# Hybrid transformer layer on one core: context keys' norm first, the merged sum's differences tile by tile, gate's rows beside another merge

## Chip, cores and metric

One core of a Trainium2 chip runs the whole kernel in one launch. Its engines work side by side, each through its own queue in order: TensorE (PE, matrix products into PSUM banks), VectorE (DVE), ScalarE (ACT), GpSimd (POOL) and SyncE (SP, which issues most DMAs). An instruction starts when those ahead of it in its queue have started and its semaphores are up, so a waiting instruction holds up all behind it. The metric is the device time of one execution in microseconds (us); smaller is better.

## What is computed

One layer over 1024 latent tokens of width 1024, with 256 context tokens as further keys. One projection feeds three branches: A, neighbourhood attention of 8 heads of 64; B, a short gated convolution; C, a Conformer convolution module with a layer norm. The branches are merged by sigmoid gates, projected and added to the input:

```python
h, gate = modulate(x, c, norm_g, w_ada, b_ada)      # gate: last third of silu(c) @ w_ada + b_ada
z = h @ w_in
kc, vc = na_kv(hc @ w_in[:, A_K:A_Z], k_norm_g)     # kc: RMS norm of the context keys, per head
...
ga, gb, gc = split(sigmoid(z[..., GATES:]), 3)
m = ga * (ya @ w_out_a) + gb * (yb @ w_out_b) + gc * (yc @ w_out_c)
x = x + gate * (m @ w_o)
```

All of it is float32. A product of two float32 matrices is made from three products of rounded parts: each operand is split into hi (a cast, on ACT) and lo (what the cast left out, a subtraction on VectorE or POOL), and hi·hi, hi·lo and lo·hi are summed in PSUM.

## The kernel before

**Order.** The program is traced in Python; when it is built, a planner puts each engine's instructions in an order by its own estimates, in which an instruction may move past others unless something holds it. `tc.issue_after(x)` is such a hold: what is traced inside it stands behind x on x's engine. Where generators are stepped beside a loop (`next(...)`), the place of tracing sets roughly where the work ends up.

**Start of attention** (about 100 to 130 us). `qkv(hp)` projects queries, keys and values of a pair of heads in eight images of 128 tokens (`ps`), and `context()` those of the 256 context tokens in two tiles (`psc`). `norm` squares a tile on ACT (`sqh`), sums it on VectorE (`ssh`), takes the power -1/2 on POOL (`rsqrt_mean`, L75 and L76) and scales on VectorE (`tm`, for the context `tmc`, L221). TensorE transposes the scaled keys (`pskc`, L194), ACT makes `kcT` of them. `attend(hp)` then prepares a head in `stacks`: VectorE's casts and differences of queries (`qd`, `qlz`, L500 to L502) and keys (`ks`, L506), `kc` of the context, and `vs` of the values (L508, POOL). POOL also fills zeros into `qlz` and `pbuf` (L481, L487), makes the low parts of the context's values (`vc`, L200) and the biases (L534). The first `qkv` runs ahead of attention, and the second, `qkv(1)`, whose images and context products TensorE computes between the first heads' scores (`sl`, `sc`), right behind the first `attend`.

**Merges** (911 us to the end). `merge(br, ys, beside)` computes for each of eight row tiles dm and two halves b a product `ops` of 12 matmuls and adds it, times the branch's gate `gs`, into `m`, held as `mt[dm]`. The order is B, A, C. Beside B's merge (`beside_b`) run A's products with its gate path (`a_steps`) and the first part of the conformer's layer norm (`norm_steps`: 32 matmuls `sums`, with the splits `lnh` and `lnl`); beside A's (`beside_a`) its end: TensorE spreads the reciprocal deviation over the partitions (`rstd`, L1113), and for each of four tiles VectorE, ACT and POOL make `cvin` (L1125) and `zcin` (L1127), split into `ych` and `ycl`, which C's merge multiplies. Beside C's merge runs `gate_steps`: one row of the condition is loaded and passed through silu (`cr`, `crs`, L1137 and L1138), and for eight tiles `gw` of the gate's weights VectorE multiplies by `crs` and sums along the row into one column of `gate` (L1143). `gs`, `zcin`, `cr`, `crs` and `gw` share eight buffers (`big`).

**m times w_o** follows C's merge in seven products per pair of row tiles instead of eight (Strassen's scheme, in Winograd's form), so sums and differences of blocks are needed. Of m: `M11`, `MT1` and `M21` inside the merge, and `MT2`, `MT3`, `M22`, `MT4` in `m_sums`, which for each of four j makes three differences `mraw` on VectorE and four splits `mb`, the cast on ACT, the low part on VectorE. Of w_o: `s1` to `s4` on POOL, and the splits `wh`, `wl`. `fin_first(n)`, a generator, makes the products `fa` and `fc` and keeps them: `pv` is a copy of `fa` on ACT (L1224), and `fc + pv` on VectorE (L1229); its second step adds `M21`'s product onto `fa`, for which the bank must have been copied, and puts the result out (`o`, L1213). `fin_rest(n)` makes `ff` (from `MT2`), `fe` (`M22`) and `fd` (`MT3`, `MT4`). `ops`, `fa`, `fc`, `ff`, `fe` and `fd` share six PSUM banks.

Of the kernel before, what the change touches and what calls it, by code (L numbers as in the profile page):

```python
# [8 lines left out]
F32 = mybir.dt.float32  # L9
F32R = mybir.dt.float32r  # L10
BF16 = mybir.dt.bfloat16
AF = mybir.ActivationFunctionType
ALU = mybir.AluOpType
AX = mybir.AxisListType
# [7 lines left out]
L = 256  # L22
EPS = 1e-6
HD = 64
# [16 lines left out]
def tile_hybrid(ctx: ExitStack, tc, x, xT, cx, cond, crow, ng, w_ada, b_ada, wqkv, wz,  # L41
                wout, wo, qg, kg, rpbs, mask, cs, cf, cfb, lng, lnb, out):
    nc = tc.nc
    pe, act, dve, pool = nc.tensor, nc.scalar, nc.vector, nc.gpsimd
# [19 lines left out]
    half_neg = cst.tile([P, 8], F32, name="half_neg")  # L64
# [8 lines left out]
    def rsqrt_mean(dst, ss, n, k):  # L73

        pool.tensor_scalar(out=dst, in0=ss, scalar1=1.0 / n, scalar2=EPS, op0=ALU.mult, op1=ALU.add)  # L75
        pool.tensor_tensor(out=dst, in0=dst, in1=half_neg[:, :k], op=ALU.pow)  # L76


    def split_chunk(src, n, lo_eng, raw=None):
# [43 lines left out]
    state = {"wp": wp}  # L123
    qg8 = cst.tile([P, 1], F32, name="qg8")
    kgn = cst.tile([P, 1], F32, name="kgn")

    def qkv(hp, w=None, cts=None, first=(), psc=None, mid=None):
# [3 lines left out]
        kcT = a1.tile([P, L], F32, tag="kcT", name="kcT")  # L131
# [37 lines left out]
        def context():  # L169
            if not state["vc"]:  # L170
                a1.tile([P, 2 * L], F32R, tag="cht", name="cht", bufs=4)
            state["vc"] = 1
            vc = [a1.tile([P, 2, P], F32R, tag=f"vc{h}", name="vc") for h in range(2)]
            pc = psc or [ps_m.tile([P, 512], F32, tag="m", name="psc"), ps_q.tile([P, 512], F32, tag="q", name="psc")]
            for k in range(KT):
                if cts:
                    cht = cts[k // 2][:, k % 2]
                else:
                    cht = a1.tile([P, 2 * L], F32R, tag="cht", name="cht", bufs=4)
                    nc.sync.dma_start(cht.bitcast(F32), chd[k])  # L180
                wh, wl = w[k][0][:, 128:384], w[k][1][:, 128:384]
                for t in range(2):
                    o = pc[t][:, :256]
                    a, b = cht[:, t * P : t * P + P], cht[:, L + t * P : L + t * P + P]
                    pe.matmul(o, a, wh, start=k == 0, stop=False)
                    pe.matmul(o, a, wl, start=False, stop=False)
                    pe.matmul(o, b, wh, start=False, stop=k == KT - 1)  # L187
            pst_ = ps_q.tile([P, 512], F32, tag="q", name="pskc")
            for t in range(2):
                tm = a1.tile([P, 256], F32, tag="tm", name="tmc", bufs=5)  # L190
                raw = a1.tile([P, 384], F32, tag="raw", name="rawc", bufs=3)
                act.copy(raw[:, :256], pc[t][:, :256])
                norm(raw[:, :P], tm[:, :P], 2)
                pe.transpose(out=pst_[:, t * P : (t + 1) * P], in_=tm[:, :P], identity=ident)  # L194
                for h in range(2):
                    hs = slice(h * HD, h * HD + HD)
                    hi, lo = vc[h][:, t, hs], vc[h][:, t, HD - h * HD : P - h * HD]
                    src = raw[:, P + h * HD : P + h * HD + HD]
                    act.copy(hi, src)
                    pool.tensor_tensor(out=lo, in0=src, in1=hi.bitcast(F32), op=ALU.subtract)  # L200
            act.activation(kcT, pst_[:, :L], AF.Identity, scale=kgn)
            return vc

        if mid:
# [9 lines left out]

    def norm(ps, dst, n):
        sq = a1.tile([P, 256], F32, tag="sqh", name="sqh", bufs=1)
        act.activation(sq[:, : n * HD], ps, AF.Square)
        ss = cst.tile([P, 4], F32, tag="ssh", name="ssh", bufs=3)
        dve.tensor_reduce(out=ss[:, :n], in_=sq[:, : n * HD].rearrange("p (h d) -> p h d", d=HD), axis=AX.X, op=ALU.add)
        rsqrt_mean(ss[:, :n], ss[:, :n], HD, n)  # L220
        dve.tensor_tensor(out=dst.rearrange("p (h d) -> p h d", d=HD), in0=ps.rearrange("p (h d) -> p h d", d=HD),  # L221
                          in1=ss[:, :n].rearrange("p (h o) -> p h o", o=1).broadcast_to([P, n, HD]), op=ALU.mult)
# [41 lines left out]
    with tc.tile_pool(name="st", bufs=1) as st, tc.tile_pool(name="ps_t", bufs=1, space=PSUM) as pst:  # L264
# [121 lines left out]
        for k in range(KT):  # L386
            raw = tmp("wraw")[:, :384]
# [77 lines left out]
    with tc.tile_pool(name="at", bufs=1, reuse_waits="tile") as at, \  # L465
# [4 lines left out]
        for hf in range(2):  # L470
            m = mka[:, hf]
            for i in range(3):
                o, n = TYPE_OFF[i], (288, 384, 288)[i]
# [10 lines left out]
        for i in range(4):  # L484
            t = at.tile([P, 768], F32, name=f"pbuf{i}")
            pad = t[:, :512].rearrange("p (j m) -> p j m", j=4)
            pool.memset(pad[:, :, 96:] if i % 2 == 0 else pad[:, :, :32], 0.0)  # L487
            pbuf.append(t)

        def stacks(hp, h):  # L490
# [104 lines left out]
        def h_sums(j):  # L595
# [16 lines left out]
            b21 = whole(0, 4 + j)  # L612
            less(3, b21, t1)

        for hp in range(4):
            attend(hp)
            if hp < 3:
                qkv(hp + 1, w1 if hp == 0 else None)
            if hp < 3:
                for j in ((), (0,), (1,))[hp]:  # L620
                    h_sums(j)
                glu(hp + 1)
# [425 lines left out]
    yc_s = []  # L1048
# [109 lines left out]
    def beside_b(dm, b):  # L1158
        if dm < 2:
            a_parts.append(a_load(2 * dm + b))  # L1160
        else:
            next(asteps, None)
        for _ in range(3 if dm > 1 else 0):
            next(steps, None)

    def beside_a(dm, b):
        for _ in range(2):
# [3 lines left out]
    merge(0, ya_s, beside_a)  # L1171
    for _ in steps:
        pass
    merge(2, yc_s, lambda dm, b: next(gsteps, None))
    for _ in gsteps:
        pass


    def m_sums():
        for j in range(4):  # L1180
            t1, b12 = halves(mt[j])
            b21, b22 = halves(mt[4 + j])
            raw = [tmp("mraw") for _ in range(3)]
            sub(dve, raw[0], b22, t1)
            sub(dve, raw[1], b22, b12)
            sub(dve, raw[2], b21, raw[0])
            for blocks, t, r in ((MT2, t2, raw[0]), (MT3, t3, raw[1])):
                blocks[j] = t[j]
                split(*t[j], r, dve)
            for blocks, tag, r in ((M22, j, b22), (MT4, 4 + j, raw[2])):  # L1190
                blocks[j] = halves(hp_pool.tile([P, S], F32R, tag=f"ha{tag}", name="mb"))
                split(*blocks[j], r, dve)
# [25 lines left out]
    def fin_first(n):  # L1218

        a11, a12, a21, a22 = w_rows(n)  # L1220
        a = fin_bank("fa")
        product(a, wsplit(a11, pool), M11, True, True)
        p1, v = held[n] = halves(big("pv"))
        act.copy(p1, a)  # L1224
        s1 = w_sum("s1", a21, a22, ALU.add)
        w12 = wsplit(a12, pool)
        c = fin_bank("fc")
        product(c, wsplit(s1, pool), MT1, True, True)
        dve.tensor_tensor(out=v, in0=c, in1=p1, op=ALU.add)  # L1229
        yield  # L1230
        xr = ltmp("xr0")
        nc.sync.dma_start(xr, xT[2 * n][:, B512[0]])
        product(a, w12, M21, False, True)
        put(2 * n, 0, a, xr)
# [28 lines left out]
    firsts = [fin_first(n) for n in range(4)]  # L1263
    for n in (0, 1):
        next(firsts[n])
    m_sums()
    for n in (0, 1, 2, 2, 3, 3):
        next(firsts[n], None)
    for n in range(4):
        fin_rest(n)  # L1270

# [83 lines left out]
```

## Time and profile before

| | us |
|---|---|
| median of three runs | 1156.2 |
| fastest, slowest run | 1153.46, 1156.84 |
| the profiled execution | 1154.55 |
| its span, first to last instruction | 1152.7 |
| TensorE busy in it | 1100.0 (95%) |
| VectorE, POOL, ACT busy | 893.1, 668.2, 569.2 |

The profile is one execution. "Idle before" an instruction is the time its engine stood still ahead of it, with the instruction that ended the wait behind the arrow. Matmuls are pipelined: one shown as 0.39 us starts 0.23 us after the one ahead of it. PEclk is the granted TensorE clock as a share of 2.4 GHz; at 1.2 GHz a matmul of 512 columns starts 0.43 us after the one ahead.

### The profile page before, as it was taken

How to read it: one execution, taken by the hardware profiler on the slowest of the kernel's cores; microseconds unless marked ns; L12 is line 12 of the kernel's file. 1: busy time of each engine (PE TensorE's matmuls, PEld its weight loads, DVE VectorE, ACT ScalarE, POOL GpSimd, SP SyncE). 2: the span in 40 equal slices, each digit the busy share in tenths (PEclk: the TensorE clock that was granted, in tenths of full speed). 3: DMA queues.
4: the chain of work that ended last, by engine and by line, in shares of the span. 5: the costliest groups of instructions: out<-in, count | busy, mean ns of one | idle time of the engine just before them, and what ended most of it. 6: DMA issues, size and time to landing. Idle time of an engine off the chain costs nothing.

```text
span 1152.7 us, 16450 instructions
## 1 busy us (share of the span) xinstructions
PE 1100.0 (95%) x5506; PEld 939.0 (81%) x5506; DVE 893.1 (77%) x1560; ACT 569.2 (49%) x1154; POOL 668.2 (58%) x611
## 2 busy tenths in 40 slices
PE   7889898999999999998999999999999999989698
PEld 5768796998999788887888888888888788878586
DVE  6976478878868885654996898897992587799975
ACT  6755366567557588784433233323434453413420
POOL 2255656446546953311968677877776645952870
PEclk7999999999999999999999999999999999999899
DMA  9536222323322323117233434344437953681263
GB/s 352 208 103 200 89 69 68 123 84 89 105 82 79 118 88 117 62 49 272 84 113 126 127 111 135 121 133 151 128 128 287 377 223 110 201 301 63 81 202 119
DMA packets 79510, 163.65 MB, mean 142 GB/s; under 512 B 10049, under 2 KB 29249, under 8 KB 79425
## 3 DMA queue, kind: packets, MB, share of 16 engines
q1 hardware_dynamic: 74816, 160.50, 41.0%
q10 hardware_dynamic: 4608, 2.10, 0.6%
q8 instruction: 43, 0.70, 0.3%
q14 instruction: 43, 0.34, 0.1%
HBM read 120.62 MB, written 41.94 MB: 141 GB/s over the span
## 4 chain that ended last, share of the span: by engine, by line
PE 71%; DVE 17%; ACT 4%; POOL 4%; issue 4%; DMA 1%; SPq 0%; ACTq 0%; POOLq 0%; DVEq 0%
PE ga L720 3%; PE gd L720 3%; PE ga L721 3%; PE gd L721 3%; PE gd L722 3%; PE ga L722 3%; PE zaps L106 3%; PE zaps L104 3%; PE zaps L105 3%; PE pp L565 2%; PE ps L106 2%; PE ps L104 2%; PE ps L105 2%; DVE mb L644 2%; PE ops L104 2%
## 5 line engine op out<-in xcount | busy, mean ns | idle before, releaser
L696 DVE SCALAR_TENSOR_TENSOR cv<-upad,cf_t,cv 128x512 f32<-128x512 f32 x240 | 167.0, 746 | 0.1
L534 POOL TENSOR_TENSOR bias<-mka,vimg 128x288 f32<-128x288 bf16 (+1 forms) x64 | 56.9, 890 | 85.7 <-DVE mn L548 81.3
L644 POOL TENSOR_TENSOR wl<-s,wh 128x512 fp32r<-128x512 f32 x69 | 98.6, 1444 | 13.8 <-ACT wh L643 13.0
L643 ACT CAST wh<-s 128x512 fp32r<-128x512 f32 x92 | 55.8, 616 | 96.1 <-POOL s L647 66.1
L87 POOL TENSOR_TENSOR wl<-wr,wh 128x384 fp32r<-128x384 f32 (+1 forms) x57 | 56.8, 1003 | 54.0 <-ACT wh L85 53.2
L570 DVE TENSOR_TENSOR plo<-pp,ph 128x512 fp32r<-128x512 f32 (+1 forms) x96 | 60.6, 639 | 7.8 <-ACT ph L568 7.1
L550 ACT ACTIVATE pbuf<-sc,mn 128x256 f32<-128x256 f32 x64 | 30.4, 476 | 73.0 <-DVE mn L548 71.5
L644 POOL TENSOR_TENSOR wl<-wr,wh 128x512 fp32r<-128x512 f32 x44 | 60.6, 1378 | 4.2 <-ACT wh L643 4.2
L565 PE MATMUL pp<-ident,pbuf 128*128 128x128 f32 x352 | 59.0, 273 | 4.0 <-DVE pbuf L554 2.8
L552 DVE TENSOR_TENSOR mn<-mn 128x1 f32<-128x1 f32 x64 | 20.0, 312 | 53.3 <-ACT pbuf L551 53.1
L720 PE MATMUL ga<-ha,wh 128*128 128x512 f32 x152 | 59.2, 390 | 1.2 <-ACT wh L643 1.2
L568 ACT CAST ph<-pp 128x512 fp32r<-128x512 f32 (+1 forms) x96 | 51.6, 549 | 15.9 <-PE pp L565 15.2
L721 PE MATMUL ga<-ha,wh 128*128 128x512 f32 x152 | 59.1, 389 | 0.0
L722 PE MATMUL ga<-ha,wl 128*128 128x512 f32 x152 | 59.1, 389 | 0.0
L565 PEld LDWEIGHTS pp<-ident,pbuf 128*128 128x128 f32 x352 | 42.6, 140 | 10.2 <-DVE pbuf L554 5.2
L748 POOL TENSOR_TENSOR s<-wr 128x512 f32<-128x512 f32 x16 | 23.3, 1454 | 38.7 <-DMA wr<-in_wz 33.3
L76 POOL TENSOR_TENSOR ssh<-ssh,half_neg 128x4 f32<-128x4 f32 (+1 forms) x40 | 41.7, 1044 | 2.9
L909 ACT ACTIVATE c<-c 128x512 f32<-128x512 f32 x18 | 11.4, 632 | 60.1 <-DVE c L726 44.5
L85 ACT CAST wh<-wr 128x384 fp32r<-128x384 f32 (+1 forms) x66 | 31.1, 486 | 18.6 <-PE psc L187 10.0
L106 PE MATMUL ps<-wh,hb 128*128 128x384 f32 x112 | 38.2, 344 | 1.2 <-DVE hb L336 1.1
L104 PE MATMUL ps<-wh,hb 128*128 128x384 f32 x112 | 38.7, 346 | 0.5 <-ACT hb L330 0.5
L548 DVE CUSTOM_DVE_ANT_0 pbuf<-sl,bias,mn 128x288 f32<-128x288 f32 (+1 forms) x64 | 36.1, 564 | 3.5 <-PE sl L543 0.4
(425 smaller groups left out, 4061.0 us busy)
## 6 DMA issues: line engine op xcount, KB each, us to landing
wr<-in_wz SPq DMA_DIRECT2D x34, 512.0 KB, 3.9
gs<-gd SPq DMA_DIRECT2D x24, 512.0 KB, 5.0
wada<-in_w_ada SPq DMA_DIRECT2D x16, 512.0 KB, 8.7
wrf<-in_wo SPq DMA_DIRECT2D x16, 512.0 KB, 4.1
wr<-in_wz SPq DMA_DIRECT2D x36, 192.0 KB, 2.5
cht<-chd SPq DMA_DIRECT2D x24, 256.0 KB, 2.9
wro<-in_wout SPq DMA_DIRECT2D x24, 256.0 KB, 4.4
gd<-gate SPq DMA_DIRECT2D x22, 256.0 KB, 3.6
```

The costliest lines, as they stand in the source:

```text
L87: lo_eng.tensor_tensor(out=lo[:, :n], in0=raw[:, :n], in1=hi[:, :n].bitcast(F32), op=ALU.subtract)
L104: pe.matmul(ps, ah, bh, start=i == 0, stop=False)
L105: pe.matmul(ps, ah, bl, start=False, stop=False)
L106: pe.matmul(ps, al, bh, start=False, stop=i == n - 1)
L534: pool.tensor_tensor(out=bv, in0=mv, in1=iv, op=ALU.subtract)
L565: pe.transpose(out=pp[:, c * 256 + hf * P : c * 256 + hf * P + P], in_=pts[hf][:, o : o + P], identity=ident)
L570: dve.tensor_tensor(out=plo[:, : m * 256], in0=pp[:, : m * 256], in1=ph[:, : m * 256].bitcast(F32), op=ALU.subtract)
L644: eng.tensor_tensor(out=lo, in0=src, in1=hi.bitcast(F32), op=ALU.subtract)
L696: dve.scalar_tensor_tensor(out=acc[b], in0=src, scalar=cf_t[:, i, j : j + 1], in1=acc[b], op0=ALU.mult, op1=ALU.add)
L720: pe.matmul(ps, wh, bh, start=first and j == 0, stop=False, skip_group_check=True)
L721: pe.matmul(ps, wh, bl, start=False, stop=False, skip_group_check=True)
L722: pe.matmul(ps, wl, bh, start=False, stop=last and j == 3, skip_group_check=True)
```

## The change

Nothing is added to or taken from the arithmetic: every engine has the same work, in another order, and the order in the middle of the kernel, from about 290 to 910 us, is the same.

```diff
@@ rsqrt_mean, norm: remember the last power, sum and square
-        pool.tensor_tensor(out=dst, in0=dst, in1=half_neg[:, :k], op=ALU.pow)
+        state["pow"] = pool.tensor_tensor(out=dst, in0=dst, in1=half_neg[:, :k], op=ALU.pow)
...
@@ context()
+            raws = []
             for t in range(2):
                 ...
                 pe.transpose(out=pst_[:, t * P : (t + 1) * P], in_=tm[:, :P], identity=ident)
+                raws.append(raw)
+            state["kc"] = state["pow"], state["red"], state["sq"]
+            act.activation(kcT, pst_[:, :L], AF.Identity, scale=kgn)
+            for t, raw in enumerate(raws):
                 for h in range(2):
                     ...
                     act.copy(hi, src)
-                    pool.tensor_tensor(out=lo, in0=src, in1=hi.bitcast(F32), op=ALU.subtract)
-            act.activation(kcT, pst_[:, :L], AF.Identity, scale=kgn)
+                    with tc.issue_after(state["kc"][0].ins):
+                        pool.tensor_tensor(out=lo, in0=src, in1=hi.bitcast(F32), op=ALU.subtract)
@@ attention
-            pool.memset(pad[:, :, 96:] if i % 2 == 0 else pad[:, :, :32], 0.0)
+            with tc.issue_after(state["kc"][0].ins):
+                pool.memset(pad[:, :, 96:] if i % 2 == 0 else pad[:, :, :32], 0.0)
...
+        with tc.issue_after(state["kc"][0].ins), tc.issue_after(state["kc"][1].ins), tc.issue_after(state["kc"][2].ins):
+            attend(0)
         for hp in range(4):
-            attend(hp)
+            if hp:
+                attend(hp)
@@ beside_b, merges
+        if dm > 2 or dm + b == 3:
+            next(gsteps, None)
...
-    merge(2, yc_s, lambda dm, b: next(gsteps, None))
     for _ in gsteps:
         pass
+    merge(2, yc_s)
@@ m_sums
-    def m_sums():
-        for j in range(4):
+    def m_sums(j):
+        with tc.issue_after(state["fin"].ins):
...
-        act.copy(p1, a)
+        state["fin"] = act.copy(p1, a)
...
-    m_sums()
-    for n in (0, 1, 2, 2, 3, 3):
-        next(firsts[n], None)
+    for j, ns in enumerate(((0, 1), (2,), (2, 3), (3,))):
+        m_sums(j)
+        for n in ns:
+            next(firsts[n], None)
```

So the two context tiles' squares, sums and powers go ahead of the first head's preparation on ACT, VectorE and POOL; gate's rows go from C's merge to the second half of B's; and the m_sums of tile j are held on ACT behind the copy `pv` that was traced last, and lie between the steps of `fin_first`.

POOL at the start of attention, before (ssh with L75 and L76 are the steps of the norm's power; the first pair is the context's):

```order
L487 MEMSET pbuf_1351 128x4x32
L200 TENSOR_TENSOR vc<-rawc,vc 128x64 x2
L534 TENSOR_TENSOR bias<-mka,vimg 128x288
L200 TENSOR_TENSOR vc<-rawc,vc 128x64 x2
L534 TENSOR_TENSOR bias<-mka,vimg 128x288
L534 TENSOR_TENSOR bias<-mka,vimg 128x384
L75 TENSOR_SCALAR ssh<-ssh 128x2
L508 TENSOR_TENSOR vs<-vb,vs 128x8x64 x2
L87 TENSOR_TENSOR wl<-wr,wh 128x384
L76 TENSOR_TENSOR ssh<-ssh,half_neg 128x2
```

and POOL at the same place now:

```order
L486 MEMSET qlz_1343 64x1024
L75 TENSOR_SCALAR ssh<-ssh 128x2
L76 TENSOR_TENSOR ssh<-ssh,half_neg 128x2
L87 TENSOR_TENSOR wl<-wr,wh 128x384
L75 TENSOR_SCALAR ssh<-ssh 128x2
L76 TENSOR_TENSOR ssh<-ssh,half_neg 128x2
L206 TENSOR_TENSOR vc<-rawc,vc 128x64 x4
L493 MEMSET pbuf_1345 128x4x32
```

Both powers moved ahead of vc, pbuf, bias and vs.

VectorE in B's merge, at the first half of dm=3, before:

```order
L1032 TENSOR_TENSOR mt_10068<-ops_10069,gs_10066 128x512
L644 TENSOR_TENSOR lnl_10177<-sq_10174,lnh_10176 128x512
L1032 TENSOR_TENSOR mt_10068<-ops_10102,gs_10066 128x512
L644 TENSOR_TENSOR wl_10563<-wro_10503,wh_10562 128x512
L644 TENSOR_TENSOR lnl_10183<-sq_10180,lnh_10182 128x512
L1032 TENSOR_TENSOR mt_10132<-ops_10133,gs_10130 128x512
```

and now (the ISA rows with gw are gate's, the others among them read the sum out):

```order
L1041 TENSOR_TENSOR mt_10075<-ops_10076,gs_10073 128x512
L1152 ISA gw_10067,gate_9901<-gw_10067,crs_10064 128x1024
L1152 ISA gate_9901 128x1
L1152 ISA gw_10110,gate_9901<-gw_10110,crs_10064 128x1024
L1152 ISA gate_9901 128x1
L1152 ISA gw_10134,gate_9901<-gw_10134,crs_10064 128x1024
L1152 ISA gate_9901 128x1
L653 TENSOR_TENSOR lnl_10193<-sq_10190,lnh_10192 128x512
L1041 TENSOR_TENSOR mt_10075<-ops_10112,gs_10073 128x512
```

Three of gate's eight rows stand ahead of the first lnl of the squares, the other five behind it; the layer norm's rows come that much later. In C's merge TensorE's order follows: before, the 21st to 24th matmul, with the last tile's parts (ych_10585, ycl_10586) in the second half of dm=0,

```order
L106 MATMUL ops_10799<-ych_10529,wl_10772 128x512
L104 MATMUL ops_10799<-ych_10585,wh_10771 128x512
L105 MATMUL ops_10799<-ycl_10586,wh_10771 128x512
L106 MATMUL ops_10799<-ych_10585,wl_10772 128x512
L104 MATMUL ops_10830<-ych_10414,wh_10824 128x512
```

and now the 38th to 42nd, behind most of dm=1 (the last tile's parts are ych_10615 and ycl_10616, and ops_10822 is dm=0's second half):

```order
L104 MATMUL ops_10822<-ych_10615,wh_10801 128x512
L105 MATMUL ops_10865<-ycl_10501,wh_10844 128x512
L106 MATMUL ops_10865<-ych_10500,wl_10845 128x512
L105 MATMUL ops_10822<-ycl_10616,wh_10801 128x512
L106 MATMUL ops_10822<-ych_10615,wl_10802 128x512
```

The last tile's products moved 16 to 18 matmuls back. ACT around the first copies pv, before (mb<-mraw are casts of m_sums):

```order
L643 CAST mb_11143<-mraw_11257 128x512
L643 CAST mb_11140<-mraw_11272 128x512
L643 CAST wh_11363<-wrf_11338 128x512
L643 CAST mb_11135<-mt_10345 128x512
L643 CAST wh_11368<-s1_11361 128x512
L1224 COPY pv_11167<-fa_11150 128x512
```

and now:

```order
L652 CAST wh_11336<-s1_11329 128x512
L1235 COPY pv_11167<-fa_11150 128x512
L652 CAST wh_11391<-wrf_11386 128x512
L652 CAST wh_11411<-wrf_11386 128x512
L1235 COPY pv_11214<-fa_11197 128x512
L652 CAST mb_11138<-mraw_11240 128x512
```

The two copies moved ahead of every cast of mraw. VectorE behind C's merge now, where before all mraw rows stood ahead of the first o:

```order
L1240 TENSOR_TENSOR pv_11214<-fc_11222,pv_11214 128x512
L653 TENSOR_TENSOR mb_11253<-mraw_11242,mb_11253 128x512
L1224 SCALAR_TENSOR_TENSOR o_11270<-fa_11150,gate_9901,xr0_11256 128x512
L1224 SCALAR_TENSOR_TENSOR o_11287<-fa_11197,gate_9901,xr0_11273 128x512
L656 TENSOR_TENSOR mraw_11290<-mt_10213,mt_9943 128x512
L656 TENSOR_TENSOR mraw_11291<-mt_10213,mt_9943 128x512
```

From mraw_11290 it is 24 rows to mb_11141, the low part of MT2's last tile.

## Rows read from the trace of the kernel before

**Rows 1.** TensorE's waits by releaser, 100 to 300 us: total us, times, longest

```profile
PE pskc L194 <- DVE tmc L221: 2.6, 1, 2.6
...
PE sl L542 <- DVE ks L506: 1.2, 1, 1.2
```

**Rows 2.** TensorE's waits by releaser, 900 us to the end

```profile
PE fa L720 <- ACT pv L1224: 8.6, 2, 5.4
PE ops L105 <- DVE ycl L644: 3.1, 1, 3.1
PE fa L721 <- DVE mb L644: 1.0, 1, 1.0
PE fd L720 <- DVE o L1213: 0.9, 1, 0.9
```

**Rows 3.** stretches: length, busy PE, PEld, DVE, ACT, POOL (count), PEclk, DMA, GB/s

```profile
115.70:130.00 14.30, 10.22 (x52) 9.42 (x51) 8.01 (x14) 4.18 (x9) 13.34 (x17) 0.88 0.10 28
911.00:962.30 51.30, 51.29 (x226) 42.49 (x227) 37.95 (x68) 23.34 (x42) 26.55 (x19) 1.00 0.64 238
1007.20:1050.70 43.50, 40.41 (x171) 32.93 (x170) 43.09 (x57) 9.22 (x16) 20.71 (x13) 0.96 0.66 226
1050.70:1094.40 43.70, 34.08 (x135) 26.73 (x134) 43.65 (x50) 18.92 (x35) 28.14 (x18) 0.89 0.23 73
1094.40:1149.00 54.60, 53.48 (x227) 43.48 (x225) 35.06 (x44) 7.21 (x12) 22.82 (x16) 0.96 0.50 169
1066.30:1078.50 12.20, 8.02 (x23) 5.54 (x22) 12.20 (x15) 5.80 (x11) 8.76 (x5) 0.72 0.12 44
1078.50:1091.70 13.20, 9.34 (x42) 7.37 (x40) 13.20 (x11) 4.03 (x8) 12.14 (x8) 0.99 0.26 79
```

**Rows 4.** timeline of TensorE: start us, us, instruction, idle before and releaser

```profile
965.56 1.02 PE L1113 MATMUL rstd<-diag,ones 128*128 128x512 f32 x2
...
1007.23 0.39 PE L104 MATMUL ops<-ych,wh 128*128 128x512 f32 x1
...
1015.47 0.50 PE L105 MATMUL ops<-ycl,wh 128*128 128x512 f32 x1 [3.09 <-DVE ycl L644]
...
1148.43 0.39 PE L722 MATMUL fd<-mb,wl 128*128 128x512 f32 x1
```

**Rows 5.** timeline of POOL at the start of attention

```profile
108.93 2.83 POOL L481 MEMSET qlz<- 64x1024 f32 x2
...
118.91 1.05 POOL L75 TENSOR_SCALAR ssh<-ssh 128x2 f32<-128x2 f32 x1
...
123.48 0.70 POOL L76 TENSOR_TENSOR ssh<-ssh,half_neg 128x2 f32<-128x2 f32 x1
```

**Rows 6.** timeline of VectorE at the start of attention

```profile
124.22 0.29 DVE L221 TENSOR_TENSOR tmc<-rawc,ssh 128x128 f32<-128x128 f32 x1 [3.08 <-POOL ssh L76]
```

**Rows 7.** VectorE: gate's rows by line (busy us, mean ns), then its timeline

```profile
L1143 DVE CUSTOM_DVE_ANT_0 gw<-gw,crs 128x1024 f32<-128x1024 f32 x8 | 13.9, 1746 | 1.7 <-POOL crs L1138 1.7
...
1015.94 1.21 DVE L1143 CUSTOM_DVE_ANT_0 gw<-gw,crs 128x1024 f32<-128x1024 f32 x1
...
1017.08 2.29 DVE L1143 CUSTOM_DVE_ANT_0 gw<-gw,crs 128x1024 f32<-128x1024 f32 x1
...
1083.66 5.16 DVE L644 TENSOR_TENSOR mb<-mraw,mb 128x512 fp32r<-128x512 f32 x3
```

**Rows 8.** timeline of POOL in A's merge and behind it

```profile
969.09 1.29 POOL L1125 TENSOR_TENSOR cvin<-cvin,lsg 128x512 f32<-128x512 f32 x1 [2.20 <-PE ops L105]
...
1004.66 2.84 POOL L1138 TENSOR_TENSOR crs<-crs,cr 128x1024 f32<-128x1024 f32 x1
1007.46 1.29 POOL L1127 TENSOR_TENSOR zcin<-zcin,cvin 128x512 f32<-128x512 f32 x1
```

**Rows 9.** timeline of ACT behind C's merge

```profile
1091.10 0.62 ACT L643 CAST mb<-mraw 128x512 fp32r<-128x512 f32 x1 [6.85 <-DVE mb L644]
...
1092.66 0.57 ACT L1224 COPY pv<-fa 128x512 f32<-128x512 f32 x1
```

More of the change, by code (lines that the diff above doesn't have):

```diff
@@ L216, in norm @@
         sq = a1.tile([P, 256], F32, tag="sqh", name="sqh", bufs=1)
-        act.activation(sq[:, : n * HD], ps, AF.Square)
+        state["sq"] = act.activation(sq[:, : n * HD], ps, AF.Square)
         ss = cst.tile([P, 4], F32, tag="ssh", name="ssh", bufs=3)
-        dve.tensor_reduce(out=ss[:, :n], in_=sq[:, : n * HD].rearrange("p (h d) -> p h d", d=HD), axis=AX.X, op=ALU.add)
+        state["red"] = dve.tensor_reduce(out=ss[:, :n], in_=sq[:, : n * HD].rearrange("p (h d) -> p h d", d=HD), axis=AX.X, op=ALU.add)
         rsqrt_mean(ss[:, :n], ss[:, :n], HD, n)
```

## Prediction

> **What bounds the kernel now.** I read the list of TensorE's waits by releaser first, since 95 parts in 100 of the span are TensorE: in the middle of the kernel, which the change leaves in its old order, nothing can be won. Two places remain. At the start of attention TensorE waits 2.6 us for tmc, the scaled context key, and 1.2 us for ks [rows 1]. From C's merge to the end it waits 8.6 us for pv, 3.1 us for ycl, 1.0 us for mb and 0.9 us for o, 13.6 in all [rows 2]. The table by stretches then says who is late there: VectorE is busy 43.09 of 43.50 us and 43.65 of 43.70 us in C's merge and behind it, and the granted clock falls to 0.96, 0.89 and 0.96, while B's merge before them has TensorE busy for all its 51.30 us at clock 1.00 and VectorE for 37.95 [rows 3].
>
> One matmul there takes 51.29 us / 226 = 0.227 us of TensorE [rows 3]. C's merge and the final products are 192 + 336 = 528 of them, 119.8 us; they took from 1007.23 to 1148.82 us, the last one's end [rows 4], 141.6 us. Of the 21.8 us more, 13.6 are waits and **8.2 us are slow matmuls** behind the three long waits, at half the clock (1.2 GHz).
>
> **The context keys' norm.** Before, POOL does the memsets of qlz and pbuf, the vc differences, biases and the vs differences ahead of the power that tmc needs: that power runs at 123.48 us, the memsets of qlz had ended at 111.76, and VectorE's tmc waits 3.08 us for it [rows 5, 6]. Now the sums, both powers and one weight split stand right behind the qlz memsets: 1.05 + 0.70 us [rows 5] put the first tmc at about 113.8 us, 10 us earlier, and the second some 3 us behind. What goes is 2.6 + 1.2 us of waits [rows 1] and slow matmuls: clock 0.88 over 14.30 us [rows 3] is 0.12 x 14.3 = 1.7 us. About 5.5 us. Nothing is removed, though, and a wait is added: VectorE now stands for POOL's first power, and its casts of queries and keys (qd, qlz, ks) are queued behind it, some 6 us later; behind POOL's second power, which waits for VectorE's second sum, stand vc, pbuf, vs and bias, and the first scores (sl) and their minimum wait for those. TensorE goes through a whole image of projections meanwhile, but the next image needs a bank that is copied out behind the same ACT and VectorE work. That wait is between nothing and the 3.8 us that it replaces; I take 2 us and 1 us of slow matmuls, so this part **gives 2.5 us** (0 to 5).
>
> **Gate's rows beside B's merge.** Eight rows (gw) of 1746 ns mean, 13.9 us, leave C's merge, where VectorE is the bound. In B's merge VectorE has 51.30 - 37.95 = 13.35 us free [rows 3, 7]. A row alone takes 1.21 us and one that meets a POOL instruction 2.29 us [rows 7]; eight are 9.7 to 18.3 us. POOL is busy only 26.55 of the 51.30 us [rows 3], so I take the lower end with a little on it: they fit, and the cover is that free time. DMA has room: share 0.64 of 51.3 us leaves 18 us, and at 238 GB/s / 0.64 = 372 GB/s the 9 loads of 0.5 MB take 12.7 us. SP's queue is passed by cr and by two pieces of weights that wait for a buffer; gs of dm=3 (multiplied into m there) stands behind that wait, and gw and gs share eight buffers. I allow **1 us lost** for a late gs (0 to 8).
>
> What the rows push back is the conformer's layer norm. In TensorE's order rstd stands 38 matmuls later: 38 x 0.227 = 8.6 us, so at 965.56 + 8.6 = 974.2 us instead [rows 4]. POOL's first cvin followed 3.5 us behind (969.09), and 25 POOL instructions later the last zcin ended at 1007.46 + 1.29 = 1008.75 [rows 8]. As many stand there now, one of 2.84 us (crs, [rows 8]) replaced by one of some 1.7: 974.2 + 3.5 + 39.7 - 1.1 = 1016.3 us. ACT's ych and VectorE's ycl then take about 0.6 and 1.7 us, as such rows do beside POOL [rows 7, 9]. TensorE reaches C's merge at 1007.2 us as before. It used to want this last ycl as its 23rd matmul, and got it at 1015.47 [rows 4], since it lay in VectorE's queue behind two gw rows. Now it wants the last ych as its 38th (1015.6 us) and the last ycl as its 41st. The old wait of 3.1 us becomes **about 2 us** (0 to 8).
>
> **m's differences tile by tile.** The 8.6 us for pv: fa is finished long before, but pv's copy stands in ACT's queue behind casts of mraw that wait for VectorE; at 1091.10 us ACT has stood 6.85 us for VectorE's mb, and pv comes at 1092.66 [rows 9]. In the new order the first two pv stand ahead of all casts of mraw, and the third behind those of the second tile only, so these waits go. What is late next is MT2's last tile. VectorE's order has two rows o in it (of fa, n = 0 and 1) that wait for TensorE's 60th and 72nd matmul behind C's merge: the second ends at 1007.2 + 2 + (192 + 72) x 0.227 + 0.4 = 1069.5 us. Then come 24 VectorE rows up to mb of MT2's last tile, which TensorE wants as its 164th matmul behind C, at 1089.8 us. The old rows were 15 in 12.2 us (0.81 each) and then 11 in 13.2 us (1.2 each) beside a busy POOL [rows 3]; 26 in 25.4 us, 0.98 each. 24 x 0.98 = 23.5 us: ready at 1093.0, **a wait of 3.2 us**. At 0.81 it is nothing, at 1.2 it is 8.5 us; a row alone has been 0.68 and one that meets POOL 1.72 (5.16 for three) [rows 7], so 24 lie between 16 and 41 us.
>
> **The sum.** Waits from C on: 2 + 3.2 + 0.9 = 6.1 us for 13.6. Slow matmuls: three long waits shared 8.2 us, 2.7 each; now one of 2.7, one short one of 1.2 and 0.5 of rest, 4.4. So 3.8 + 7.5 = 11.3 us gained there, 2.5 at the start, 1 lost in B's merge: 12.8 us. The profiled execution is 1154.55 us and would be 1141.75; the median of the three runs is 1156.2, 1.65 above it. I add half of that: **1142.5 us**.
>
> **Rivals.** (a) *All waits go*: the layer norm and MT2 are just in time, the start of attention gives 5 us, B's merge loses nothing. That is 3.2 + 2 + 3.9 of slow matmuls + 2.5 + 1 = 12.6 us more, 1130. For it: the last ych misses its matmul by 1.3 us only, and 24 rows at 0.81 would be in time. Against: it needs both.
> (b) *The layer norm is late*, because a POOL chain of 25 instructions shifts by 8.6 us with nothing to spare. TensorE waits 8 us at C's start instead of 2, and 1.5 more of slow matmuls: 1150. For it: POOL never stood still in those 39.7 us. Against: VectorE, which POOL meets there, no longer has gw rows.
> (c) *B's merge is held up*, by gate rows of 2.29 us (18.3 us for 13.35 free) or by gs behind gw in SP's queue: 5 to 8 us, 1148 to 1151.
> (d) *MT2's chain meets POOL throughout, and the kernel gets slower.* Place: the 24 VectorE rows behind the second o. Price: 1.72 us each, 41 us, so ready at 1110.8 for 1089.8: a wait of 21 us instead of 3.2, 1142.5 + 17.8 = 1160. It decides from the mean row: the gain is used up where the wait is 3.2 + 13.7 = 16.9, at (1089.8 + 16.9 - 1069.5) / 24 = 1.55 us. For it: three rows in turn did take 1.72 while POOL was busy 12.14 of 13.20 us [rows 3, 7]. Against: that same stretch had 1.2 on average, and POOL can work ahead while VectorE now stands waiting for the two o.
> The Trainium skill, "SBUF — State Buffer", section "Who interferes with whom", has the rule behind (d): a VectorE instruction with two inputs in SBUF and a GpSimd instruction that reads SBUF exclude each other for the whole instruction, and who comes first holds the ports. Rows of 1.21 and 2.29 us for one kind of instruction agree with it. By that rule alone each of the 24 rows could meet a POOL instruction, which is (d)'s 1160.
>
> **How the numbers follow.** Forecast, 1136 to 1149: 0.55. (a) 0.12. (b) 0.13. (c) 0.10. (d) 0.06; nothing gained on balance, from (b) and (c) together, 0.04. A measurement of this kernel tells 0.3%, about 3.5 us, from no change. Faster by more holds the forecast, (a), and most of (b) and (c): 0.81. Within: 0.10. Slower: 0.09. The range runs from 1132, where (a) is nearly whole, to 1154, where (b) and (c) add up.
>
> **What would show it.** Right: no wait for pv of over 1 us; tmc ahead of 118 us and no 2.6 us wait in front of pskc; eight gw rows before 962 us with a mean near 1.3 us; a wait for ycl or ych of 0 to 4 us at C's start and one of 0 to 9 us at the first ff. Wrong: waits of TensorE inside B's merge, where there were none; a zcin after 1020 us; gw rows near 2.3 us; rows of over 1.4 us on average between the second o and ff; a new wait of over 4 us, with a fallen clock, before an image of projections.

## Result, and the profile after

| | before | after |
|---|---|---|
| median of four runs each, same chip | 1156.52 us | 1142.53 us |
| fastest, slowest | 1153.46, 1157.74 | 1141.50, 1143.65 |
| profiled execution (span) | 1154.55 (1152.7) | 1142.37 (1140.6) |
| first matmul of B's merge | 911.01 | 907.47 |
| B's and A's merge | 96.22 | 96.21 |
| C's first matmul to the last matmul's end | 141.59 | 132.98 |

The ratio is 0.9883, 95% interval 0.9862 to 0.9905: 14 us faster by medians, 12.2 between the two profiled executions. Of the 12.1 us between the two spans, 3.5 are won ahead of B's merge, none in B's and A's, 8.6 behind. This is one execution against one; further traces of the same orders, below, put more ahead of B's merge and less behind.

Waits of TensorE in the changed kernel from 900 us on (releaser, total, times, longest), to be held against [rows 2]:

```profile
PE fa L729 <- ACT pv L1235: 3.9, 1, 3.9
PE fe L730 <- DVE mb L653: 1.9, 1, 1.9
PE fd L729 <- DVE o L1224: 0.9, 1, 0.9
PE ops L104 <- ACT ych L652: 0.9, 2, 0.5
...
PE ops L105 <- DVE ycl L653: 0.6, 1, 0.6
PE ff L730 <- DVE mb L653: 0.3, 1, 0.3
```

Six causes from C's merge on, 8.5 us, where there were 13.6 (0.8 us for px ahead of B's merge is there before and after). Pv still leads. The stretches of the changed kernel, columns as in [rows 3]: B's merge, C's merge, to the first ff, to the end:

```profile
907.50:958.80 51.30, 51.30 (x226) 42.48 (x227) 43.87 (x68) 24.57 (x42) 28.94 (x19) 1.00 0.88 321
...
1003.70:1049.60 45.90, 44.40 (x193) 35.78 (x192) 42.45 (x50) 11.82 (x21) 25.00 (x17) 1.00 0.43 141
1049.60:1088.90 39.30, 35.40 (x146) 28.79 (x145) 34.08 (x34) 16.62 (x30) 26.57 (x17) 0.91 0.38 122
1088.90:1136.70 47.80, 44.63 (x193) 35.54 (x191) 38.58 (x48) 8.01 (x14) 20.66 (x13) 1.00 0.40 137
```

B's merge takes gate's rows (VectorE 37.95 to 43.87 us) in the same 51.3 us, TensorE still without a gap. C's merge now takes 45.9 us from its first matmul to the first fa; before it was 48.5.

The waits of the changed kernel from 100 to 300 us, for [rows 1] (plo's is at 191 us, the others before 134):

```profile
PE ps L104 <- ACT raw L144: 1.3, 1, 1.3
PE sl L548 <- DVE mn L554: 1.1, 1, 1.1
PE pp L571 <- DVE plo L576: 0.9, 1, 0.9
PE sc L546 <- DVE kc L510: 0.8, 1, 0.8
```

Its timeline there, one row each of POOL, VectorE and ACT, for [rows 5, 6]:

```profile
112.35 0.70 POOL L76 TENSOR_TENSOR ssh<-ssh,half_neg 128x2 f32<-128x2 f32 x1
...
113.09 1.10 DVE L226 TENSOR_TENSOR tmc<-rawc,ssh 128x128 f32<-128x128 f32 x1 [2.01 <-POOL ssh L76]
...
123.96 0.42 ACT L222 ACTIVATE sqh<-raw 128x256 f32<-128x256 f32 x1 [5.88 <-DVE ssh L224]
```

The power runs at 112.35 instead of 123.48 us, and the waits for tmc and ks are gone. In their place TensorE waits 1.3 us for a bank of an image (raw), whose copy stands on ACT behind a square that waited 5.88 us for VectorE; then for kc and mn.

### The profile page after: what moved, and what is told of

It is laid out like the page before. It is cut to its first block, busy times and chain, and to the rows that moved or that the text cites. A ratio compares the mean times of both kernels' runs of the same rounds, so it can differ in the third digit from the quotient of the medians.

```text
span 1140.6 us, 16449 instructions
## 1 busy us (share of the span) xinstructions
PE 1095.6 (96%) x5506; PEld 937.8 (82%) x5506; DVE 892.1 (78%) x1560; ACT 568.2 (50%) x1154; POOL 667.1 (58%) x611
## 4 chain that ended last, share of the span: by engine, by line
PE 73%; DVE 10%; ACT 5%; POOL 5%; issue 4%; DMA 2%; SPq 1%; ACTq 0%; DVEq 0%; POOLq 0%
PE ga L729 3%; PE gd L729 3%; PE ga L730 3%; PE gd L730 3%; PE gd L731 3%; PE ga L731 3%; PE pp L571 3%; PE ps L106 2%; PE ps L104 2%; PE ops L105 2%; PE ops L104 2%; PE ps L105 2%; PE ops L106 2%; PE zaps L106 2%; PE zaps L104 2%
## 5 line engine op out<-in xcount | busy, mean ns | idle before, releaser
L87 POOL TENSOR_TENSOR wl<-wr,wh 128x384 fp32r<-128x384 f32 (+1 forms) x57 | 56.6, 998 | 53.9 <-ACT wh L85 53.2
L574 ACT CAST ph<-pp 128x512 fp32r<-128x512 f32 (+1 forms) x96 | 51.7, 548 | 16.9 <-PE pp L571 16.3
L76 POOL TENSOR_TENSOR ssh<-ssh,half_neg 128x4 f32<-128x4 f32 (+1 forms) x40 | 43.2, 1080 | 3.1
```

The costliest lines, as they stand in the source:

```text
L87: lo_eng.tensor_tensor(out=lo[:, :n], in0=raw[:, :n], in1=hi[:, :n].bitcast(F32), op=ALU.subtract)
```

## Experiments

Four runs took the change apart on one chip: each of its three parts alone on top of the kernel before, and two of them together. Theory A: VectorE's load bounds C's merge and what follows, so moving gate's rows carries the gain there, and the order of m's differences gives little. The rival, the prediction's: that order frees pv and carries most.

**The start alone** (the hunks of the change up to attention, nothing else):

```diff
...
+            state["kc"] = state["pow"], state["red"], state["sq"]
+            act.activation(kcT, pst_[:, :L], AF.Identity, scale=kgn)
+            for t, raw in enumerate(raws):
...
+        with tc.issue_after(state["kc"][0].ins), tc.issue_after(state["kc"][1].ins), tc.issue_after(state["kc"][2].ins):
+            attend(0)
         for hp in range(4):
-            attend(hp)
+            if hp:
+                attend(hp)
```

> Only the first part of the change: the context keys' norm ahead of attention's preparation. Theory (the three parts add up): the start of attention gains 5 to 6 us by 360 us of the trace, as between the two kernels, and nothing behind it changes, so 1156.5 - 4.5 (between 3.5 and 6), about 1152; the granted clock may or may not fall behind the 1.9 us wait for ya near 520 us, which is worth 1.5 us. Rival (the norm only moves the wait): under 2 us gained, 1155 or more.

**Gate's rows alone:**

```diff
+        if dm > 2 or dm + b == 3:
+            next(gsteps, None)
...
-    merge(2, yc_s, lambda dm, b: next(gsteps, None))
     for _ in gsteps:
         pass
+    merge(2, yc_s)
```

> Only gate's rows beside B's merge instead of C's. Theory A (VectorE's load bounds the tail): C's merge is relieved of 13.9 us of rows and 1.7 us of waiting, so ycl, the differences and the casts that pv stands behind all come earlier, and most of the tail's gain is here: 6 to 9 us, 1148 to 1150. Theory B (the order of ACT's queue bounds the tail): pv still stands behind all casts of mraw, only the wait for ycl shrinks from 3.1 to 1.5 us with its slow matmuls: 2 to 4 us, 1153 to 1154. B's and A's merges take 96.2 us together as before in both.

**The differences alone:**

```diff
+        with tc.issue_after(state["fin"].ins):
...
-    m_sums()
-    for n in (0, 1, 2, 2, 3, 3):
-        next(firsts[n], None)
+    for j, ns in enumerate(((0, 1), (2,), (2, 3), (3,))):
+        m_sums(j)
+        for n in ns:
+            next(firsts[n], None)
```

> Only m's differences tile by tile. Theory A (VectorE's load): pv comes early, but VectorE is still some 12 us behind, now also standing for the rows o, so the wait moves to MT2's last tile at ff and is as long: within 3 us of before, 1153 to 1160. Theory B (the order of ACT's queue): the two waits for pv, 8.6 us, and their slow matmuls go but for some 3 us: 5 to 8 us, 1148 to 1151.

**Both of these** (the last two diffs together):

> Gate's rows and the differences, without the start of attention. If the parts add up: the whole change without the start's gain, 1142.5 + 4.5 = 1147 (1146 to 1148.5), with 8.6 us less between C's first matmul and the last one than the 141.6 us of before. If the start's earlier end matters for the tail: more than 1149.

| | median us | ratio, 95% interval | C to the end, profiled |
|---|---|---|---|
| start alone | 1145.96 | 0.9932 [0.9913, 0.9951] | 137.93 |
| gate alone | 1146.89 | 0.9942 [0.9922, 0.9962] | 132.62 |
| differences alone | 1154.00 | 0.9999 [0.9987, 1.0012] | 139.93 |
| gate and differences | 1148.58 | 0.9959 [0.9944, 0.9974] | 133.38 |

(The kernel before had 1154.16 us there.) Theory A holds. The differences' order gives nothing alone, and on top of gate's move nothing either (the medians are 1.7 us apart the other way, and their intervals overlap). By the ratios the start gives 7.8 us and gate's move 6.7, which make up the 14. That the start gives 7.8 was in neither theory, and it is outside the 3.5 to 6 expected; see below.

The last column needs care, since each number is one execution. The kernel before, the start alone and the start without the hold (below) have one and the same order on TensorE, VectorE, ACT and POOL from C's merge on, and they took 141.59, 137.93 and 139.57 us from C to the end: 139.7 on the mean. The two with gate's move and the differences in the old order took 132.62 and 130.99, 7.9 less; the three with both changes 132.98, 133.42 and 133.38, 6.4 less. So all that the whole change wins in the tail is gate's move, and the differences' order on top of it leans to a cost: 1.5 us between these means, 1.7 us between the medians here and 2.0 in the next table. No single one of these comparisons shows that cost.

Four more runs asked what the tail is still bound by.

**The changed kernel again**, as the yardstick of that chip:

> The changed kernel once more, beside the three others of this call. 0.988 of before. It fixes what the next kernels are compared with on one chip, and shows whether the granted clock falls behind the 1.9 us wait for ya near 520 us in this execution too.

**Start and gate without the differences** (against the changed kernel):

```diff
...
-    for j, ns in enumerate(((0, 1), (2,), (2, 3), (3,))):
-        m_sums(j)
-        for n in ns:
-            next(firsts[n], None)
+    m_sums()
+    for n in (0, 1, 2, 2, 3, 3):
+        next(firsts[n], None)
```

> The change without m's differences tile by tile (m_sums as before). Theory (the differences' order gives nothing, VectorE's load was the bound): C's first matmul to the last one takes 132 to 133.5 us as in the whole change, and the time is within 3 us of the whole change, on either side. Rival (the parts add up as medians of the single kernels: start 0.9932, gate 0.9942, and the differences cost 2 us on top of gate): 2 us faster than the whole change, 0.986 of before. Rival (the differences gain once the start is earlier): 3 us or more slower than the whole change.

**The third and fourth pv a step earlier** (against the changed kernel):

```diff
-    for j, ns in enumerate(((0, 1), (2,), (2, 3), (3,))):
+    for j, ns in enumerate(((0, 1, 2), (2, 3), (3,), ())):
```

> The whole change, with the third fa and its copy pv traced, on ACT, ahead of the second tile's differences, so that the copy no longer stands behind casts of mraw. Theory (the 3.9 us wait for pv is ACT's queue order): it goes with some 2.7 us of slow matmuls behind it, and half of that comes back at ff or fe, whose last tile is no earlier: 2 to 5 us less than the whole change from C's first matmul to the last. Rival (VectorE's rows set the end of MT2 and M22 whatever ACT does): the wait moves to ff or fe, within 1 us of the whole change.

**POOL's sums s1 to s4 left out** (against the changed kernel; the first operand of each sum stands in its place, so the products are of other weights):

```diff
-        t = bp.tile([P, 512], F32, tag=("lnh", "lnl")[state["ws"] % 2], name=name, bufs=3)
-        pool.tensor_tensor(out=t, in0=a, in1=b, op=op)
-        return t
+        return a
```

> The whole change with the sums s1 to s4 of w_o's blocks on POOL left out (their first operand is used in their place, so the products are of other weights); TensorE, ACT and VectorE do as much as before, POOL 16 instructions of about 1.6 us less. Theory (VectorE's rows are slow where they meet POOL): the 24 rows between the second o and MT2's last tile take 0.8 us instead of 1.13, the waits for pv, ff and fe (6 us) go and with them slow matmuls: C's first matmul to the last one 126 to 129 us instead of 133. Rival (VectorE's rows wait for ACT or buffers rather than for POOL): 131.5 us or more.

| (before 1154.92 us) | median us | ratio, 95% interval | C to the end |
|---|---|---|---|
| changed kernel again | 1141.96 | 0.9887 [0.9868, 0.9907] | 133.42 |
| start and gate | 1139.93 | 0.9865 [0.9844, 0.9885] | 130.99 |
| pv earlier | 1140.65 | 0.9881 [0.9859, 0.9903] | 133.45 |
| no sums on POOL | 1131.26 | 0.9794 [0.9777, 0.9811] | 123.70 |

Taking the wait for pv away by order alone did not shorten the tail (133.45 us for 133.42). Two tails ended below what was expected: start and gate at 130.99 us (132 to 133.5), and without POOL's sums 123.70 (126 to 129). TensorE's waits with pv earlier:

```profile
PE fd L729 <- DVE o L1224: 2.3, 1, 2.3
PE fe L730 <- DVE mb L653: 1.8, 1, 1.8
PE ff L730 <- DVE mb L653: 1.4, 2, 0.7
PE ff L731 <- POOL wl L653: 1.4, 1, 1.4
```

The 3.9 to 4.3 us for pv are gone and stand again in front of fd and ff. With POOL's sums out, VectorE's work of 1060 to 1085 us by line (busy us, mean ns, idle before):

```profile
L653 DVE TENSOR_TENSOR mb<-mraw,mb 128x512 fp32r<-128x512 f32 x9 | 7.5, 852 | 2.9 <-ACT mb L652 2.8
L656 DVE TENSOR_TENSOR mraw<-mt 128x512 f32<-128x512 f32 x6 | 3.8, 682 | 0.0
```

and the two longest of TensorE's waits from C's merge on:

```profile
PE ops L105 <- DVE ycl L653: 1.2, 1, 1.2
PE fd L729 <- DVE o L1222: 0.9, 1, 0.9
```

The same instructions are quick, VectorE even stands idle, every wait for pv or mb is gone, and the tail is 9.7 us shorter than the 133.42 of the changed kernel on that chip. Leaving the sums out also takes away results that others could wait for; that the rows are drawn out beside POOL is in the changed kernel's own trace. POOL stands still from 1084.69 to 1091.41 us:

```profile
1091.41 1.66 POOL L653 TENSOR_TENSOR wl<-s,wh 128x512 fp32r<-128x512 f32 x1 [6.72 <-issue]
```

and of two VectorE rows of one kind, the first stands beside POOL's work, the second in that gap:

```profile
1083.49 1.75 DVE L653 TENSOR_TENSOR mb<-mraw,mb 128x512 fp32r<-128x512 f32 x1
...
1085.77 0.68 DVE L653 TENSOR_TENSOR mb<-mraw,mb 128x512 fp32r<-128x512 f32 x1
```

So most of what the changed kernel's tail has beyond its 528 matmuls at 0.227 us (9.7 of 13.6 us) is VectorE's rows drawn out beside POOL's sums; reordering did not take it away.

The last four runs asked what in the start part gives the 8 us, whether holding only later tiles gets the waits back, and whether the place of gate's rows matters (before: 1154.27 us there).

**The start part without the hold** (against the start alone; the holds on `vc` and `pbuf` stay):

```diff
-        with tc.issue_after(state["kc"][0].ins), tc.issue_after(state["kc"][1].ins), tc.issue_after(state["kc"][2].ins):
-            attend(0)
         for hp in range(4):
-            if hp:
-                attend(hp)
+            attend(hp)
```

> Only the start part, and of it only the order in which the program is written (kcT and the context's squares ahead of vc); the hold of the first attend(0) behind the norm's square, sum and power is left out, and the one on vc and pbuf too where it hung on it. If the written order alone carries the start's gain, then as start_alone: 1146, ratio about 0.993, the last heads' row 5 to 7 us earlier than before. If it is the hold that puts the powers ahead of the first heads' preparation, then tmc stays behind attention's casts, TensorE's wait in front of pskc of 1 to 3 us stays, and the time is 1151 to 1156 (0.995 to 1.000). Which: mostly the hold, 1152.

**Later tiles held** (against start and gate; `m21` is the low part of M21's last tile):

```diff
...
-    m_sums()
+    m_sums(range(1))
+    with tc.issue_after(state["fin"].ins), tc.issue_after(m21.ins):
+        m_sums(range(1, 4))
```

> Start and gate parts as in start_and_gate; m's differences in one block, but those of the tiles j = 1, 2 and 3 held on VectorE behind the last split of M21 and on ACT behind the copy pv of n = 1, so that the first two pv and the first two o can't stand behind casts of mraw. If the waits for pv (1.4 us in start_and_gate, 3.9 in the changed kernel) and mb (3.6 us) can be had by order, C's merge to the end takes 127 to 129 us for start_and_gate's 130.99, and the time is 1136 to 1138, 0.983 to 0.985. If VectorE's rows beside POOL set the end whatever their order, it stays at 130 to 133 us: 1139 to 1142.

**Only the last two tiles held** (the same with `range(2)` and `range(2, 4)`):

> As hold_later_tiles with the hold on j = 2 and 3 alone, so that VectorE can make two tiles ahead of M21's products. By order: between start_and_gate and hold_later_tiles, 1136 to 1139. By VectorE's load: 1139 to 1142, no different from start_and_gate.

**Gate's rows beside A's merge** (against start and gate):

```diff
@@ beside_b
-        if dm > 2 or dm + b == 3:
-            next(gsteps, None)
@@ beside_a
+        next(gsteps, None)
```

> Start part as in start_and_gate, m's differences in one block, but gate's eight rows beside A's merge instead of the second half of B's. If only VectorE's load in C's merge and behind it counts, it is start_and_gate again: 1140, C's merge to the end 131 us. If the free time that takes the rows in has to be free of POOL as well, then it is worse: A's merge has 44.9 - 35.6 = 9.3 us of VectorE free and POOL busy for 39 of 45 us there, so eight rows near 1.75 us are 14 us, the layer norm's last zcin comes late, and TensorE waits 4 to 8 us at C's start, or in A's merge: 1143 to 1148. The latter is the likelier.

| | median us | ratio, 95% interval | C to the end |
|---|---|---|---|
| start without hold | 1154.06 | 0.9993 [0.9983, 1.0004] | 139.57 |
| later tiles held | 1140.45 | 0.9876 [0.9858, 0.9893] | 132.55 |
| last two tiles held | 1141.37 | 0.9886 [0.9868, 0.9904] | 134.67 |
| gate's rows beside A's merge | 1143.66 | 0.9902 [0.9886, 0.9918] | 135.72 |

The hold carries the start's gain; written order alone gives at most 2 us. Holding the tiles failed: with later tiles held, mb's and pv's waits of start and gate (3.6 and 1.4 us) are one,

```profile
PE fa L729 <- ACT pv L1236: 6.1, 1, 6.1
```

and the sum of waits from C on is 8.5 us for 7.3. Of all versions start and gate has the lowest median, 1139.93, but its interval overlaps those of the changed kernel, pv earlier and both held ones: none is shown to beat the changed kernel. Its four runs (1137.34 to 1140.50) all lie below the changed kernel's four on that chip (1140.73 to 1143.63), which makes it likely.

Gate's rows beside A's merge (min, median, max ns, then first and last start):

```profile
L1152 DVE CUSTOM_DVE_ANT_0 gw<-gw,crs x8: 1211/1226/1708, 939.7 to 987.8; 128x1024 f32<-128x1024 f32 x8
```

and TensorE's waits of that run from C's start on, with one for rstd in A's merge:

```profile
PE ops L104 <- ACT ych L652: 2.6, 1, 2.6
...
PE ops L105 <- DVE ycl L653: 1.1, 1, 1.1
PE fd L729 <- DVE o L1223: 0.9, 1, 0.9
PE rstd L1122 <- DVE diag L1116: 0.5, 1, 0.5
```

The time came as expected (1143 to 1148), but not by the rows near 1.75 us that the expectation priced (median 1.23). The layer norm's chain has the rows among its own now, and VectorE, in whose queue they stand, waits five times for their loads:

```profile
DVE gw L1152 <- DMA gw<-in_w_ada: 10.3, 5, 3.3
```

In start and gate no gw row waits for its load. TensorE waits 2.6 + 1.1 us at C's start where start and gate has 0.8 + 0.6, and B's and A's merges take 97.53 us instead of 96.23. By the ratio to before it is 0.9902 for 0.9865, about 4 us slower. So the place counts, by what stands behind the rows in the queue and by how late their loads come, and not by what a row takes; the run does not part these two.

## Why the prediction was right, and where its working was not

The time was right (1142.5 forecast, 1142.53 measured), but by two errors of opposite sign: the start gave more than its term, the tail less, and the tail's credit was with the wrong part of the change. That they cancel so closely is luck.

**The start: term mis-sized, because the prediction priced only its first 20 us.** The -2.5 us hold for what it looked at. VectorE's first row of `pbuf` (the first head's scores) starts at 133.9 to 135.0 us in the four traces without the start part and at 130.9 to 133.4 in the nine with the held one, 2.4 us earlier on the mean. The new wait before an image that the term allows came, 1.3 us, though without a fall of the clock (1.00 from 110 to 134 us). What it missed lies 50 us later, and a line of it stood in the list of [rows 1], second, between the two that the prediction took:

```profile
PE py L575 <- DVE plo L570: 1.6, 1, 1.6
```

VectorE of the kernel before, when it prepares the next heads:

```profile
180.87 1.50 DVE L500 CAST qd<-qT 64x1024 fp32r<-64x1024 f32 x1
182.41 1.30 DVE L501 CAST qd<-qT 64x1024 fp32r<-64x1024 f32 x1
183.74 1.22 DVE L502 TENSOR_TENSOR qlz<-qT,qd 64x1024 fp32r<-64x1024 f32 x1
...
186.02 0.41 DVE L570 TENSOR_TENSOR plo<-pp,ph 128x256 fp32r<-128x256 f32 x1
```

TensorE's row that waits for this plo:

```profile
186.49 0.39 PE L575 MATMUL py<-plo,vc 128*128 128x256 f32 x1 [1.62 <-DVE plo L570]
```

and the stretch, columns as in [rows 3]:

```profile
174.70:191.00 16.30, 13.98 (x78) 11.08 (x76) 13.72 (x24) 13.11 (x24) 8.30 (x7) 1.00 0.30 89
```

Two casts and a difference stand in the chain from scores to plo, and TensorE idles 2.3 of the 16.3 us. The changed kernel has them 9 us earlier. Two of its rows on VectorE:

```profile
173.47 1.30 DVE L507 CAST qd<-qT 64x1024 fp32r<-64x1024 f32 x1
174.81 1.22 DVE L508 TENSOR_TENSOR qlz<-qT,qd 64x1024 fp32r<-64x1024 f32 x1
```

and its stretch, with 0.4 us of TensorE idle:

```profile
175.00:191.00 16.00, 15.60 (x84) 12.91 (x83) 12.32 (x26) 14.25 (x28) 10.68 (x9) 1.00 0.13 38
```

From the first to the eleventh row of scores written to `pbuf` it is 56.6 to 56.8 us in the kernel before, gate alone and differences alone, 51.8 in the changed kernel, the start alone and later tiles held: 4.9 us won, of which 1.0 on the mean is lost again by the last such row. Without the hold it is 56.2, and the wait for plo is back:

```profile
183.75 0.39 PE L581 MATMUL py<-plo,vc 128*128 128x256 f32 x1 [1.63 <-DVE plo L576]
```

Without the hold the context's first power is late as well:

```profile
119.95 0.70 POOL L76 TENSOR_TENSOR ssh<-ssh,half_neg 128x2 f32<-128x2 f32 x1
```

and TensorE waits 2.0 us for tmc and 1.7 for ks. So the hold made most of the start's gain, and the larger part of it at a place that it doesn't name: the planner put the next heads' casts elsewhere. Why it did is not shown, nor what the earlier power alone would give, since both go with the hold. Without it the first `pbuf` row is early too (131.56 us), and yet the median gains nothing; its profiled execution is the fastest of twelve, 2.4 us under their median, so its trace can't say where the others lose it, and that stays open. Over all nine traces with the held start, the last row of scores stands at 505.7 to 509.3 us, in the four without any of it at 513.3 to 514.5: 6.4 us between the means, against the 2.5 forecast. At B's first matmul it is 6.7 (905.8 for 912.5).

**B's merge: right, 1 us allowed and none lost.** The changed kernel's gate rows (min, median, max), beside [rows 7]:

```profile
L1152 DVE CUSTOM_DVE_ANT_0 gw<-gw,crs x8: 1208/1212/1707, 934.0 to 950.4; 128x1024 f32<-128x1024 f32 x8
```

Seven of eight run at the undisturbed 1.21 us and one at 1.71; rival (c) fell.

**The layer norm: right.** rstd comes at 970.64 us (965.56 in [rows 4]), 63.2 us behind B's first matmul instead of 54.6: the 8.6 us later that 38 matmuls cost. The last zcin ended at 1012.70 (1008.75 by [rows 8]), 105.2 us behind B's first matmul (forecast 105.3). The waits at C's start are 0.9 + 0.6 = 1.5 us, forecast 2, for 3.1 before; rival (b) fell.

**pv: the step that failed.** "So these waits go" counted the first three copies and not the fourth. ACT of the changed kernel and TensorE behind it:

```profile
1081.92 0.62 ACT L652 CAST mb<-mraw 128x512 fp32r<-128x512 f32 x1 [3.40 <-DVE mb L653]
...
1082.97 0.58 ACT L1235 COPY pv<-fa 128x512 f32<-128x512 f32 x1
...
1083.60 0.80 PE L729 MATMUL fa<-mb,wh 128*128 128x512 f32 x1 [3.90 <-ACT pv L1235]
```

The first three copies (1055.50, 1058.33 and 1071.51) are in time. The fourth stands behind a cast of the second tile's mraw, that cast behind VectorE, and VectorE behind POOL. It is the wait of [rows 9] once more, smaller, and of the prediction's signs of being right it is the one that did not come ("no wait for pv of over 1 us"). And the gain that was put down to the new order came from VectorE having eight rows less in C's merge: the differences alone gave 0.9999.

**MT2's last tile: mechanism right, row mis-sized.** VectorE of the changed kernel from the second o to ff, by line:

```profile
L653 DVE TENSOR_TENSOR mb<-mraw,mb 128x512 fp32r<-128x512 f32 x8 | 10.1, 1286 | 0.0
L656 DVE TENSOR_TENSOR mraw<-mt 128x512 f32<-128x512 f32 x6 | 6.3, 1069 | 1.7 <-DMA out<-o 1.7
L656 DVE TENSOR_TENSOR mraw<-mt,mraw 128x512 f32<-128x512 f32 x3 | 4.2, 1400 | 0.0
...
L1240 DVE TENSOR_TENSOR pv<-fc,pv 128x512 f32<-128x512 f32 x2 | 1.4, 676 | 0.0
```

The 24 rows start at 1066.80, and ff was let go at 1093.68: 1.12 us a row, where the prediction took 0.98 and rival (d) decides from 1.55. In it are 1.7 us (without them 1.05 a row) that no term had: mraw takes its buffers in turn with o, and o now stands between the tiles, so one difference waits until o is written out. Because TensorE had lost 3.9 us to pv just before, ff itself waits only 0.3, and fe 1.9 behind it; together 2.2 us, for 3.2 forecast. So rival (a), no waits at all, fell too.

Rows that read a PSUM bank (`fc`, 0.68 us, the second of them at 1091.84 beside a POOL row) are not drawn out, those with both inputs from SBUF are, to 1.07 to 1.40 on average, and without POOL's sums the same mraw takes 0.68. The Trainium skill, "SBUF — State Buffer", section "Who interferes with whom", says it so: a VectorE instruction with at most one SBUF input (and outside its two-port modes) doesn't contend with GpSimd. The trace agrees, by these means. By its rule (d)'s mechanism is at work; its price was too high, since POOL is busy 26.57 of 39.30 us, not throughout.

**The sum of the tail.** 528 matmuls at 0.227 us are 119.8 us; 132.98 less that is 13.2, of which 8.5 are waits (forecast 6.1) and the other 4.7 are put down to slow matmuls (forecast 4.4). So -8.6 came for -11.3: the 2.7 missing are the fourth pv, set off in part by MT2 and C's start.

**What nearly cancelled.** Start -3.5 at B's first matmul (-2.5 forecast), B's merge 0.0 (+1), tail -8.6 (-11.3): -12.1 of span for -12.8. Over all traces of the same orders both errors are larger: -6.7 for the start and -6.4 for the tail.

## What to carry to other kernels

Where one engine's load bounds a stage, move work off it into one where it has time; reordering what stays only renamed the wait here, four times. And a hold or a move in a planned order has to be followed through the stages behind it, by the engine's rows and not only at the place edited: more than half of this start's gain lay 50 us later. Taking a change apart, part by part, is the only thing here that showed whose gain it was.

## What was not expected of the hardware

One and the same wait of TensorE costs 1.5 us more in some executions. In attention's end TensorE stands 1.93 us for ya in every kernel here. TensorE's timeline in the kernel before:

```profile
523.22 0.39 PE L574 MATMUL py<-ph,vs 128*128 128x256 f32 x1 [1.93 <-DVE ya L578]
```

and its 8 us behind that wait, columns as in [rows 3]:

```profile
523.20:531.20 8.00, 7.98 (x39) 6.79 (x40) 1.45 (x3) 1.31 (x4) 0.16 (x2) 1.00 0.59 210
```

The same row in the changed kernel:

```profile
518.19 0.39 PE L580 MATMUL py<-ph,vs 128*128 128x256 f32 x1 [1.93 <-DVE ya L584]
```

and its 8 us behind it:

```profile
518.20:526.20 8.00, 8.00 (x33) 6.79 (x34) 1.42 (x3) 0.39 (x2) 0.16 (x2) 0.79 0.53 185
```

Same instructions and same wait, yet the granted clock is 1.00 in one and 0.79 in the other (a mean: part of the stretch ran at 1.2 GHz), and 39 matmuls become 33. It is 1.00 in eight traces here and 0.79 in six, and the changed kernel, profiled twice, has one of each. From ya's matmul to B's first one it is 387.79 us before and 389.28 after: 1.5 us that the change did not cause and that hide a part of the start's gain in the two profiled executions. So slow matmuls behind this wait are a chance, not a price, and two single traces can't be compared below some 2 us in the middle of the kernel, nor in the tail, where one and the same order took 137.93 to 141.59 us, below some 4 us.
